# The MLP norm's factor applied with the ReLU by one vector instruction, and paired products that read the input times the norm's weights alone

## The chip, the cores and the metric

The kernel runs on one core of one Trainium2 chip. The metric is the time of one execution on the device in microseconds (us). The kernel before was timed three times; the profiled execution is one more.

## The reference

A decoder trunk of two layers on one sequence of 512 tokens with 1024 features. Each layer has a mixer half and an MLP half; the change lies in the MLP half.

```
def rms_norm(x, g):
    y = xf * lax.rsqrt(jnp.mean(xf * xf, axis=-1, keepdims=True) + NORM_EPS)
    return (y * g.astype(jnp.float32)).astype(x.dtype)
...
for l in range(DEPTH):
    h = rms_norm(x, norm_mix_g[l])
    proj = h @ w_in[l]
    ...
    x = x + mixed @ w_out[l]
    h = rms_norm(x, norm_mlp_g[l])
    x = x + jnp.square(jax.nn.relu(h @ w_mlp_up[l])) @ w_mlp_down[l]
return rms_norm(x, final_norm_g)
```

`mixed` puts together differential attention (6 heads), a short convolution and RWKV-7 (6 heads). `w_mlp_up` is 1024 x 4096, `w_mlp_down` 4096 x 1024. The norm's factor is one positive number for each token, `norm_mlp_g` one number for each feature.

## The kernel before

**Storage and precision.** Activations are kept transposed: `x[j]`, j = 0 to 7, are eight tiles of 128 features x 512 tokens in float32. Every product runs in the matmul type fp32r with each operand split into a high and a low part, and takes three matmuls for each 128 rows of the contraction: high weight by high input, high weight by low input, low weight by high input. So each tensor has an instruction that rounds to the high part (on ScalarE, ACT) and one that subtracts it to get the low part (on VectorE, DVE, or GpSimd, POOL). Weights come from memory by DMAs on SyncE's queue as tiles `raw` (128 x 512), and are split into `whi` (ACT) and `wlo` (DVE, in the mixer half on DVE or POOL as a table has it).

**Order of the work.** In the mixer half the order in which instructions are issued is written out in tables. The MLP half is written as plain code in program order. A scheduler with its own cost model then sets the order on each engine, and may put instructions of the MLP half ahead of instructions that were issued before them, where their inputs and their buffers allow it.

**The end of the mixer half.** The output projection makes eight tiles `po`, in two cuts of four steps of the contraction. DVE adds each to `x[j]` (L715). Of each finished `x[j]`, ACT makes the square (L738, L741), and DVE or POOL, by a table, adds the squares up in `accf` (L744). ACT makes `ahif[j]`, the high part of `x[j]` times the norm's weights (L730), and DVE the low part `alof[j]` (L731). These 16 tiles are the input of the up products: the norm's factor isn't in them. `inner_norm` (L746 to L761) makes the factor: TensorE (PE) sums `accf` over the features (`pssf`), DVE adds the epsilon and scales (`rsx`, L359), POOL raises to the power -0.5 (`rrf`, L363), PE spreads the result over the partitions (`prbf` in PSUM, L757), and ACT copies it into SBUF (`rs`, L761; the trace names its buffer `rsf`). Before, the code kept both `rs` and its copy in PSUM, `rb`.

**The up stage.** The MLP half has 32 up products of 128 outputs. The first eight (`N_ONE`) are ordinary: 24 matmuls of 128 x 512 each, `up_0` to `up_7`. The first three of them are issued with the mixer half. `up(i)` multiplies the sums in PSUM by the norm's factor (`c = up * rs`, DVE, L1402), and `square` takes the ReLU (ACT, L1389) and the square (ACT, L1391). `kept` splits that into `mh` (ACT, L1381) and `ml` (POOL, L1382).

**Inputs of the paired products.** The other 24 up products are made in twelve pairs. For them, during the up stage, `scaled_by_norm(j)` makes `bn[j]`, the normed input: `x[j]` times weights times `rb` (DVE, L1415, reading `rb` from PSUM). `blocks(k)` makes of `bn[k]` and `bn[k + 4]` four sums `t` on halves of the tokens (DVE, L1421 to L1424) and splits them into `thi` (ACT, L1428) and `tlo` (DVE, L1429). `parts_of(j)`, called in the first down products, splits `bn[j]` into `bhi` (ACT, L1437) and `blo` (DVE, L1438). These go into the buffers of `ahif` and `alof`, and so must wait until the last ordinary up product has read those.

**The paired stage.** `two(i0, i1)` makes two up products at once from seven block products in place of eight, each of 12 matmuls of 128 x 256 (a Strassen scheme in Winograd's form: `pa`, `pb`, `pc` are their sums in PSUM). Sums of weight blocks (`s1` to `s4`, DVE, L1458) are split by `both` (ACT L1452, DVE L1453). Three of the products read halves of the normed input (`blk`, from `bhi`/`blo`), four the sums (`smm`, from `thi`/`tlo`). DVE puts the results together into `c0` and `c1`, and `square` is called for the first product of the pair with `[c0]` and for the second with `[pa, c1]`.

**The down products.** `down(h, js)` contracts four squared tiles: for each of eight `j`, 12 matmuls of 128 x 512 into a bank `dn` of PSUM, and DVE adds them to `x[j]` (L1514). After each pair four of these stand in program order, so that a pair and 48 matmuls of `down` make one step. The last part of layer 1 is made by `last_group` (`dnF`).

Of the kernel before, what the change touches and what calls it, by code (L numbers as in the profile page):

```python
# [10 lines left out]
F32 = mybir.dt.float32  # L11
F32R = mybir.dt.float32r
# [3 lines left out]
AF = mybir.ActivationFunctionType  # L16
ALU = mybir.AluOpType
# [5 lines left out]
S = 512  # L23
P = 128
NK = D // P
# [153 lines left out]
N_ONE = 8  # L179
# [7 lines left out]
C_GMIX, C_GMLP, C_SUB, C_CONV, C_MU = 0, 8, 16, 17, 23  # L187
# [81 lines left out]
def tile_trunk(ctx: ExitStack, tc: tile.TileContext, xT, wts, prm_d, cst_d, lora_d, gup_d, lam_d, fin_d, out):  # L269
    nc = tc.nc  # L270
    act, dve, pool = nc.scalar, nc.vector, nc.gpsimd
# [22 lines left out]
    cp = Pool(ctx.enter_context(tc.tile_pool(name="cp", bufs=1)), "cp")  # L294
# [10 lines left out]
    x = [cp.tile([P, S], F32, tag=f"x{j}", name=f"x{j}") for j in range(NK)]  # L305
# [58 lines left out]
    nrm = {}  # L364
# [28 lines left out]
    acts = {}  # L393
# [169 lines left out]
    for l in range(L):  # L563
        pr = prm[l]
# [4 lines left out]
        with ExitStack() as mx:  # L569
# [176 lines left out]
            def inner_norm():  # L746
                key = f"f{l}"
                yield from got(nrm, "all" + key)
                pt = psum("rp", 4, f"pss{key}")
                for b in range(NB):  # L750
                    ins = pe.matmul(pt[:, b:b + 1], nrm[key][0][:, b * P:(b + 1) * P], ones1, start=True, stop=True)
                yield ins
                r = cp.tile([P, NB], F32, tag="rr", bufs=2, name=f"rr{key}")
                yield from root_steps(r, pt[:, :NB], NB)
                rb = psum("rp", 4, f"prb{key}")
                for b in range(NB):
                    ins = pe.matmul(rb[:, b * P:(b + 1) * P], r[:, b:b + 1].to_broadcast([P, P]), ident, start=True, stop=True)  # L757
                yield ins
                rs = cp.tile([P, S], F32, tag="rs", bufs=1, name=f"rs{key}")
                nrm["rs"] = rs, rb  # L760
                yield act.copy(rs, rb)  # L761

            def norm():
# [604 lines left out]
        with ExitStack() as mx:  # L1368
# [2 lines left out]
            H = S // 2  # L1371
            mids = []

            rs, rb = nrm["rs"]

            def kept(m):

# [7 lines left out]
            def square(cs, name):  # L1385

                r = fp.tile([P, S], F32, tag="r", bufs=2, name=f"r{name}")
                for i, c in enumerate(cs):
                    act.activation(r[:, i * H:i * H + c.shape[1]], c, AF.Relu)  # L1389
                m = fp.tile([P, S], F32, tag="m", bufs=3, name=f"m{name}")  # L1390
                act.activation(m, r, AF.Square)  # L1391
                kept(m)

            def up(i):

                if i < NUP:
                    pt = ups[i]
                else:
                    pt = psum("rp", 4, f"up{l}_{i}")
                    mm3(pt, weights(wbase + NG_IN + NG_OUT + i), acts)  # L1400
                c = fp.tile([P, S], F32, tag="c0", bufs=2, name=f"c{l}_{i}")
                dve.tensor_tensor(c, pt, rs, ALU.mult)  # L1402
                square([c], f"{l}_{i}")

            bn, th = {}, {}

            def scaled_by_norm(j):
                if j == 0:  # L1410
                    fp.tile([P, 8], F32, tag="pad0", name=f"pad0_{l}")
                bn[j] = fp.tile([P, 2, H], F32, tag="shi" if j < 5 else "slo", bufs=5, name=f"bn{l}_{j}")
                if j == 5:
                    fp.tile([P, 24], F32, tag="pad1", name=f"pad1_{l}")
                dve.scalar_tensor_tensor(bn[j].rearrange("p a s -> p (a s)"), x[j], pr[:, C_GMLP + j:C_GMLP + j + 1], rb,  # L1415
                                         ALU.mult, ALU.mult)

            def blocks(k):
                b1, b2 = bn[k], bn[k + 4]
# [6 lines left out]
                for i in range(2):  # L1426
                    u = slice(2 * i, 2 * i + 2)
                    act.copy(hi[:, u], t[i])  # L1428
                    dve.tensor_tensor(lo[:, u], t[i], hi[:, u].bitcast(F32), ALU.subtract)  # L1429

            bs = {}

            def parts_of(j):

                n = 1 if j < 4 else 2
                hi, lo = bs[j] = [cp.tile([P, 2, H], F32R, tag=f"a{p}{j}", name=f"b{p}{l}_{j}") for p in ("hi", "lo")]
                act.copy(hi[:, :n], bn[j][:, :n])  # L1437
                dve.tensor_tensor(lo[:, :n], bn[j][:, :n], hi[:, :n].bitcast(F32), ALU.subtract)  # L1438

            def two(i0, i1):  # L1440

                n = f"{l}_{i0}"
                wg = wbase + NG_IN + NG_OUT

                def raw(i, a):
                    t = fp.tile([P, 4, P], F32, tag="sraw", bufs=6, name=f"raw{n}_{i}_{a}")
                    nc.sync.dma_start(t.rearrange("p k c -> p (k c)"), wts[wg + i, :, a * P:(a + 4) * P])
                    return t

                def both(src, name):  # L1450
                    hi, lo = [fp.tile([P, 4, P], F32R, tag=f"s{p}", bufs=5, name=f"s{p}{n}_{name}") for p in ("hi", "lo")]
                    act.copy(hi, src)  # L1452
                    dve.tensor_tensor(lo, src, hi.bitcast(F32), ALU.subtract)  # L1453
                    return hi, lo

                def sum_(name, a, b, op):
                    t = fp.tile([P, 4, P], F32, tag=name, name=f"{name}{n}")
                    dve.tensor_tensor(t, a, b, op)  # L1458
                    return t

                def small(name):
                    return fp.tile([P, H], F32, tag=name, bufs=2, name=f"{name}{n}")

                def product(pt, w, moving, first=True):

                    whi, wlo = w
                    for k in range(4):
                        ahi, alo = moving(k)
                        pe.matmul(pt, whi[:, k], ahi, start=(first and k == 0), stop=False, skip_group_check=True)
                        pe.matmul(pt, whi[:, k], alo, start=False, stop=False, skip_group_check=True)  # L1470
                        pe.matmul(pt, wlo[:, k], ahi, start=False, stop=(k == 3), skip_group_check=True)

                blk = lambda d, q: lambda k: [p[:, q] for p in bs[4 * d + k]]
                smm = lambda q: lambda k: [p[:, q] for p in th[k]]
                pa, pb = [psum("rp", 4, f"p{i}{n}")[:, :H] for i in "ab"]
                pc = psum("at", 2, f"pc{n}")[:, :H]
                c0 = fp.tile([P, S], F32, tag="c0", bufs=2, name=f"c0{n}")
                w11 = raw(i0, 0)
                product(pa, both(w11, "p1"), blk(0, 0))
                p1 = small("p1")  # L1480
                act.copy(p1, pa)
                w21 = raw(i1, 0)
                w22 = raw(i1, 4)
                s1 = sum_("s1", w21, w22, ALU.add)
                product(pb, both(s1, "p5"), smm(0))
                p5 = small("p5")
                dve.tensor_copy(p5, pb)
                s2 = sum_("s2", s1, w11, ALU.subtract)
                product(pa, both(s2, "p6"), smm(1), False)
                u2 = small("u2")  # L1490
                act.copy(u2, pa)
                w12 = raw(i0, 4)
                product(pc, both(w12, "p2"), blk(1, 0))
                dve.tensor_tensor(c0[:, :H], pc, p1, ALU.add)
                s3 = sum_("s3", w11, w21, ALU.subtract)
                product(pa, both(s3, "p7"), smm(2), False)
                c1 = small("c1")
                dve.tensor_tensor(c1, pa, p5, ALU.add)
                s4 = sum_("s4", w12, s2, ALU.subtract)
                product(pb, both(s4, "p3"), blk(1, 1), False)  # L1500
                dve.tensor_tensor(c0[:, H:], pb, u2, ALU.add)
                square([c0], f"{n}_0")
                product(pa, both(w22, "p4"), smm(3), False)
                square([pa, c1], f"{n}_1")

            def down(h, js):

                g, k0 = h // 2, 4 * (h % 2)
                for j in js:
                    pt = psum("mm", 2, f"dn{l}_{h}_{j}")  # L1510
                    mm3(pt, weights(wbase + NG_IN + NG_OUT + NG_UP + 8 * g + j, k0, k0 + 4), mids[4 * h:4 * h + 4], 4)
                    if h == 0:
                        parts_of(j)
                    dve.tensor_tensor(x[j], pt, x[j], ALU.add)  # L1514
                    if h == 2 * N_KG - 1 and j < NK - LATE:
                        norm_tile(j, f"m{l + 1}")


            for i in range(N_ONE):
                up(i)  # L1520
                for j in range(2 * max(i - 2, 0), min(2 * max(i - 1, 0), NK)):
                    scaled_by_norm(j)
                if i >= N_ONE - 4:
                    blocks(i - N_ONE + 4)
            down(0, range(NK))
            h, half = 1, 0
            for p in range(N_TWO):
# [76 lines left out]
```

## Time and profile before

| what | value |
|---|---|
| time before, median of 3 | 1255.2 us (1253.98 to 1256.6) |
| time of the profiled execution | 1255.07 us |
| its span in the trace | 1253.1 us |
| granted TensorE clock, mean | 0.997 |
| moved by DMA | 127.92 MB, 102 GB/s |
| one paired step (a pair and 48 `dn` matmuls) | 21.0 us |

The page lists for each engine its busy time and share of the span. In rows of the trace the first number is the start in us from the span's start, the second the duration; then come engine, line, operation and the tiles, written as out<-in. A bracket at the end of a row gives the idle time of the engine just before it and the instruction that ended that time. In lists of waits each line gives the waiting group, what it waited for, the total in us, the number of waits and the longest one. The ordinary up products of layer 0 run from about 281 to 325 us and those of layer 1 from about 897 to 946; the twelve steps with pairs of layer 1 run from 968 to 1197.

### The profile page before, as it was taken

The numbers are of one execution on the slowest core, as the hardware profiler recorded it, in microseconds if no ns is written. First come the engines' busy times: TensorE is split into PE (matmuls) and PEld (weight loads), VectorE is DVE, ScalarE is ACT, GpSimd is POOL, SyncE is SP. The second block draws the span as 40 slices with busy tenths as digits, with TensorE's granted clock in tenths as the row PEclk, the third lists the DMA queues.
The fourth block names the chain that finished last, engine by engine and source line by source line (L and its number), as shares of the span: only waits on it lengthen the run. The fifth ranks groups of instructions, "written<-read, shape, count | busy, mean of one in ns | idle before, by whom it ended". The sixth has DMA issues, their size and how long they took to land. (4 is left out here: it accounts for less than half of the span.)

```text
span 1253.1 us, 25011 instructions
## 1 busy us (share of the span) xinstructions
PE 1233.6 (98%) x9493; PEld 1055.0 (84%) x9493; DVE 903.3 (72%) x1731; ACT 697.5 (56%) x1476; POOL 358.2 (29%) x461
## 2 busy tenths in 40 slices
PE   9999999999999999999999999999999999999997
PEld 6888788788799999999778887888878999998987
DVE  6887888768967676764666777887598666666654
ACT  6785655546645454544475656464565545454553
POOL 1264637332301010101225455464221111111100
PEclk9999999999999999999999999999999999999998
DMA  6523323142332323221235233232423232323122
GB/s 214 162 91 93 113 87 107 53 143 84 128 100 94 110 93 110 93 93 35 78 109 161 80 119 108 91 88 71 141 84 135 93 109 94 108 95 108 53 76 76
DMA packets 84696, 127.92 MB, mean 102 GB/s; under 512 B 21472, under 2 KB 25568, under 8 KB 84576
## 3 DMA queue, kind: packets, MB, share of 16 engines
q1 hardware_dynamic: 83856, 125.77, 31.4%
q8 instruction: 75, 1.23, 0.4%
q10 hardware_dynamic: 720, 0.55, 0.1%
q14 instruction: 45, 0.37, 0.1%
HBM read 117.11 MB, written 9.18 MB: 101 GB/s over the span
## 5 line engine op out<-in xcount | busy, mean ns | idle before, releaser
L1382 POOL TENSOR_TENSOR ml<-m,mh 128x512 fp32r<-128x512 f32 x64 | 93.4, 1461 | 500.7 <-ACT mh L1381 482.7
L338 ACT CAST whi<-raw 128x512 fp32r<-128x512 f32 x142 | 88.0, 621 | 174.4 <-PE dn L282 159.0
L282 PE MATMUL dn<-mh,whi 128*128 128x512 f32 x448 | 175.1, 391 | 1.2 <-DVE x L1514 1.2
L282 PE MATMUL dn<-ml,whi 128*128 128x512 f32 x448 | 174.6, 390 | 0.0
L282 PE MATMUL dn<-mh,wlo 128*128 128x512 f32 x448 | 174.6, 390 | 0.0
L674 POOL TENSOR_TENSOR wlo<-raw,whi 128x512 fp32r<-128x512 f32 x84 | 110.5, 1316 | 189.2 <-ACT whi L662 159.4
L282 PE MATMUL pj<-ahim,whi 128*128 128x512 f32 x392 | 156.6, 399 | 1.0 <-DVE x L1514 0.9
L282 PE MATMUL pj<-ahim,wlo 128*128 128x512 f32 x392 | 156.7, 400 | 0.0
L282 PE MATMUL pj<-alom,whi 128*128 128x512 f32 x392 | 156.0, 398 | 0.0
L662 ACT CAST whi<-raw 128x512 fp32r<-128x512 f32 x142 | 87.5, 617 | 85.8 <-PE pj L282 29.8
L1514 DVE TENSOR_TENSOR x<-dn,x 128x512 f32<-128x512 f32 x112 | 76.7, 686 | 77.4 <-PE dn L282 77.4
L339 DVE TENSOR_TENSOR wlo<-raw,whi 128x512 fp32r<-128x512 f32 x142 | 113.4, 799 | 11.3 <-ACT whi L338 10.7
L1453 DVE TENSOR_TENSOR slo_p<-s,shi_p 128x512 fp32r<-128x512 f32 x96 | 70.9, 741 | 63.4 <-ACT shi_p L1452 60.8
L282 PEld LDWEIGHTS dn<-mh,whi 128*128 128x128 f32 x448 | 84.1, 188 | 19.9 <-issue 2.0
L282 PEld LDWEIGHTS dn<-mh,wlo 128*128 128x128 f32 x448 | 84.1, 188 | 17.9
L282 PEld LDWEIGHTS dn<-ml,whi 128*128 128x128 f32 x448 | 84.1, 188 | 16.5
L1452 ACT CAST shi_p<-s 128x512 fp32r<-128x512 f32 x96 | 59.1, 617 | 49.7 <-PE pa L282 38.1
L282 PEld LDWEIGHTS pj<-ahim,whi 128*128 128x128 f32 x392 | 73.8, 188 | 15.1 <-ACT whi L662 1.3
L282 PEld LDWEIGHTS pj<-alom,whi 128*128 128x128 f32 x392 | 73.9, 189 | 14.0 <-issue 0.5
L282 PEld LDWEIGHTS pj<-ahim,wlo 128*128 128x128 f32 x392 | 73.8, 188 | 14.0 <-DVE wlo L674 0.2
L282 PE MATMUL pa<-tlo,shi_p 128*128 128x256 f32 x288 | 81.4, 282 | 0.0
L282 PE MATMUL pa<-thi,shi_p 128*128 128x256 f32 x288 | 81.2, 282 | 0.0
(416 smaller groups left out, 3232.5 us busy)
## 6 DMA issues: line engine op xcount, KB each, us to landing
raw<-wts SPq DMA_DIRECT2D x389, 256.0 KB, 2.7
qs<-dqhi SPq DMA_DIRECT2D x24, 128.0 KB, 3.7
ks<-dkhi SPq DMA_DIRECT2D x24, 128.0 KB, 4.0
x<-xT SPq DMA_DIRECT2D x8, 256.0 KB, 4.6
dqhi<-qhi SPq DMA_DIRECT2D x6, 256.0 KB, 3.3
dqlo<-qlo SPq DMA_DIRECT2D x6, 256.0 KB, 3.4
dkhi<-khi SPq DMA_DIRECT2D x6, 256.0 KB, 2.7
dklo<-klo SPq DMA_DIRECT2D x6, 256.0 KB, 3.5
```

Of the source, the lines that this page charges most:

```text
L282: ins = nc.tensor.matmul(*a, **k)
L338: act.copy(hi[:, :n], raw[:, :n])
L339: (pool if a and lean[0] else dve).tensor_tensor(lo[:, :n], raw[:, :n], hi[:, :n].bitcast(F32), ALU.subtract)
L662: yield act.copy(hi[:, k0:k1], raw[:, k0:k1])
L674: yield eng.tensor_tensor(lo[:, k0:k1], raw[:, k0:k1], hi[:, k0:k1].bitcast(F32), ALU.subtract)
L1382: pool.tensor_tensor(lo, m, hi.bitcast(F32), ALU.subtract)
L1452: act.copy(hi, src)
L1453: dve.tensor_tensor(lo, src, hi.bitcast(F32), ALU.subtract)
L1514: dve.tensor_tensor(x[j], pt, x[j], ALU.add)
```

## The change

- `square` no longer has ACT take the ReLU. One DVE instruction (`scalar_tensor_tensor`) takes the larger of its input and 0 and multiplies by the norm's factor `rs`, straight into `r`. The factor is positive, so ReLU first and factor second give the same as the other way round. ACT's square and everything behind it stay.
- `up` gives the sums in PSUM to `square` directly; its multiplication `c` is gone.
- The input of the paired products no longer has the norm's factor in it. `by_gain(j)` takes the place of `scaled_by_norm(j)`: ACT makes `bn[j]` as `x[j]` times the norm's weights, which needs neither the norm's factor nor `rb` in PSUM. It is called with `blocks`, which itself stays the same. One buffer's place and a padding move (`bn[4]` from `shi` to `slo`).
- `parts_of` is gone: what the products read in `bhi`/`blo` are now halves of `ahif`/`alof`, which hold the same without the factor.
- In a pair `square` now applies the factor to `c0`, `pa` and `c1`: three DVE instructions where ACT took three ReLUs.

```diff
@@ inner_norm
-                nrm["rs"] = rs, rb
+                nrm["rs"] = rs
@@ square
                 for i, c in enumerate(cs):
-                    act.activation(r[:, i * H:i * H + c.shape[1]], c, AF.Relu)
+                    q = slice(i * H, i * H + c.shape[1])
+                    dve.scalar_tensor_tensor(r[:, q], c, 0.0, rs[:, q], ALU.max, ALU.mult)
@@ up
-                c = fp.tile([P, S], F32, tag="c0", bufs=2, name=f"c{l}_{i}")
-                dve.tensor_tensor(c, pt, rs, ALU.mult)
-                square([c], f"{l}_{i}")
+                square([pt], f"{l}_{i}")
@@
-            def scaled_by_norm(j):
+            def by_gain(j):
+
                 if j == 0:
                     fp.tile([P, 8], F32, tag="pad0", name=f"pad0_{l}")
-                bn[j] = fp.tile([P, 2, H], F32, tag="shi" if j < 5 else "slo", bufs=5, name=f"bn{l}_{j}")
-                if j == 5:
+                bn[j] = fp.tile([P, 2, H], F32, tag="shi" if j < 4 else "slo", bufs=5, name=f"bn{l}_{j}")
+                if j == 4:
                     fp.tile([P, 24], F32, tag="pad1", name=f"pad1_{l}")
-                dve.scalar_tensor_tensor(bn[j].rearrange("p a s -> p (a s)"), x[j], pr[:, C_GMLP + j:C_GMLP + j + 1], rb,
-                                         ALU.mult, ALU.mult)
+                act.activation(bn[j].rearrange("p a s -> p (a s)"), x[j], AF.Identity, scale=pr[:, C_GMLP + j:C_GMLP + j + 1])
@@
-            def parts_of(j):
-
-                n = 1 if j < 4 else 2
-                hi, lo = bs[j] = [cp.tile([P, 2, H], F32R, tag=f"a{p}{j}", name=f"b{p}{l}_{j}") for p in ("hi", "lo")]
-                act.copy(hi[:, :n], bn[j][:, :n])
-                dve.tensor_tensor(lo[:, :n], bn[j][:, :n], hi[:, :n].bitcast(F32), ALU.subtract)
@@ two
-                blk = lambda d, q: lambda k: [p[:, q] for p in bs[4 * d + k]]
+                blk = lambda d, q: lambda k: [p[:, q * H:(q + 1) * H] for p in acts[4 * d + k]]
@@ down
-                    if h == 0:
-                        parts_of(j)
@@ the loop of the first eight
                 up(i)
-                for j in range(2 * max(i - 2, 0), min(2 * max(i - 1, 0), NK)):
-                    scaled_by_norm(j)
                 if i >= N_ONE - 4:
-                    blocks(i - N_ONE + 4)
+                    k = i - N_ONE + 4
+                    by_gain(k)
+                    by_gain(k + 4)
+                    blocks(k)
```

Besides, the order that the scheduler makes differs: the prediction shows the places on which it rests, in rows of the two programs' instruction order.

More of the change, by code (lines that the diff above doesn't have):

```diff
@@ L1372, in tile_trunk @@
             mids = []
-            rs, rb = nrm["rs"]
+            rs = nrm["rs"]
             def kept(m):
@@ L1429, in blocks @@
                     dve.tensor_tensor(lo[:, u], t[i], hi[:, u].bitcast(F32), ALU.subtract)
-            bs = {}
-            def parts_of(j):
-                n = 1 if j < 4 else 2
-                hi, lo = bs[j] = [cp.tile([P, 2, H], F32R, tag=f"a{p}{j}", name=f"b{p}{l}_{j}") for p in ("hi", "lo")]
-                act.copy(hi[:, :n], bn[j][:, :n])
-                dve.tensor_tensor(lo[:, :n], bn[j][:, :n], hi[:, :n].bitcast(F32), ALU.subtract)
             def two(i0, i1):
```

## The prediction

> **What bounds the kernel now.** I read the page's busy times first, then the waits of PE, then PE row by row where a wait stands.
>
> ```profile
> PE 1233.6 (98%) x9493; PEld 1055.0 (84%) x9493; DVE 903.3 (72%) x1731; ACT 697.5 (56%) x1476; POOL 358.2 (29%) x461
> ```
> ```profile
> PE dn L282 <- DVE x L1514: 1.2, 3, 0.7
> ...
> PE up L282 <- DVE wlo L339: 0.9, 1, 0.9
> ...
> PE up L282 <- ACT whi L338: 0.5, 1, 0.5
> ...
> PE up L282 <- DVE bn L1415: 0.4, 1, 0.4
> ```
> TensorE is busy for 98% of the span, so an edit elsewhere counts only where PE then waits less or more. The second fence (total us, times, longest) holds the waits that the edited code could touch: three in the up products of layer 1, and one of 0.7 in layer 0's first down products, where DVE is late with `x` while it makes the `blo` parts. The change can win little more than these. Their full cost includes the slow restart of PE:
>
> ```profile
> 915.38 0.39 PE L282 MATMUL up<-alof,whi 128*128 128x512 f32 x1
> 915.61 0.39 PE L282 MATMUL up<-ahif,wlo 128*128 128x512 f32 x1
> 916.53 0.50 PE L282 MATMUL up<-ahif,whi 128*128 128x512 f32 x1 [0.53 <-ACT whi L338]
> 916.86 0.40 PE L282 MATMUL up<-alof,whi 128*128 128x512 f32 x1
> 918.14 0.50 PE L282 MATMUL up<-ahif,wlo 128*128 128x512 f32 x1 [0.88 <-DVE wlo L339]
> ...
> 920.32 0.39 PE L282 MATMUL up<-ahif,wlo 128*128 128x512 f32 x1
> 921.09 0.47 PE L282 MATMUL up<-ahif,whi 128*128 128x512 f32 x1 [0.38 <-DVE bn L1415]
> 921.40 0.40 PE L282 MATMUL up<-alof,whi 128*128 128x512 f32 x1
> ```
> Undisturbed matmuls start 0.23 apart. From 915.61 to 921.40 there are 14 steps, worth 3.2; they took 5.8, so **2.6 us** are lost here.
>
> **The change, part by part.** *The paired stage (two thirds of the MLP).* Each pair gains three vector instructions `r` and loses three ReLUs on ACT.
>
> ```profile
> 970.00:1180.00 210.00, 210.00 (x1329) 190.84 (x1328) 143.81 (x232) 104.56 (x201) 27.33 (x20) 1.00 0.30 99
> ```
> ```profile
> L731 DVE SCALAR_TENSOR_TENSOR alof<-x,prm,ahif x16: 743/746/1752, 263.4 to 902.1; 128x512 fp32r<-128x512 f32 x16
> ...
> L730 ACT ACTIVATE ahif<-x,prm x16: 707/710/726, 262.6 to 901.0; 128x512 fp32r<-128x512 f32 x16
> ```
> ```profile
> L1402 DVE TENSOR_TENSOR c<-up,rsf x16: 675/679/692, 291.8 to 947.3; 128x512 f32<-128x512 f32 x16
> ```
> Columns of the first: stretch, its length, then busy time of PE, PEld, DVE, ACT, POOL. In ten steps of 21.0 us PE never idles, and DVE has 66.2 us free, 6.6 a step. The new `r` has no row; its nearest are `alof` (0.75) and `c` (0.68), so a whole one and two half ones take at most 1.5 a step, and fit. Cost 0; ACT's relief is worth 0 as well. The first eight up products trade `c` plus a ReLU for one `r` of `c`'s size: 0. On the path this costs something only without cover, between the last two pairs of layer 1, where no down group stands: at most 1.5.
>
> *What is taken from the up stage.* Eight `bn` and eight `blo` instructions leave DVE there, and the sums `t`/`tlo` move to earlier places. The PE queue of layer 1 moves with them; first before, then after, at the end of the third up product:
>
> ```order
> L282 MATMUL up_2_11687<-ahif_7_11627,wlo_4_11673 128x512
> L282 MATMUL up_4_11803<-ahif_0_11418,whi_0_11806 128x512
> L282 MATMUL up_4_11803<-alof_0_11419,whi_0_11806 128x512
> L282 MATMUL up_4_11803<-ahif_0_11418,wlo_0_11807 128x512
> L282 MATMUL up_4_11803<-ahif_1_11446,whi_0_11806 128x512
> ```
> ```order
> L282 MATMUL up_2_11639<-ahif_7_11579,wlo_4_11625 128x512
> L282 MATMUL up_3_11693<-ahif_0_11370,whi_0_11696 128x512
> L282 MATMUL up_3_11693<-alof_0_11371,whi_0_11696 128x512
> L282 MATMUL up_3_11693<-ahif_0_11370,wlo_0_11697 128x512
> L282 MATMUL up_3_11693<-ahif_1_11398,whi_0_11696 128x512
> ```
> Half of `up_4`, whose weights were not split yet, no longer stands ahead of `up_3`, and no `bn` holds the bank of `prbf`. I count both layers' stalls as won: **-2.6** and, with 0.1 of restart, **-0.8**.
>
> *What is put ahead of the up stage.* In layer 1, DVE's rows between the last additions of the output projection (`x`) and the first `alof`, before and after; `t`, `tlo` are the sums for the pairs, `thi_1` comes from ACT:
>
> ```order
> L715 TENSOR_TENSOR x_74<-po_5_4_11509,x_74 128x512
> L744 TENSOR_TENSOR accf_11416<-accf_11416,sqf_5_11539 128x512
> L715 TENSOR_TENSOR x_75<-po_6_4_11532,x_75 128x512
> L715 TENSOR_TENSOR x_76<-po_7_4_11554,x_76 128x512
> L731 SCALAR_TENSOR_TENSOR alof_2_11573<-x_71,prm_67,ahif_2_11572 128x512
> ```
> ```order
> L715 TENSOR_TENSOR x_75<-po_6_4_11484,x_75 128x512
> L1421 TENSOR_TENSOR t_1_0_11850<-bn_5_11848,t_1_0_11850 128x256
> L1422 TENSOR_TENSOR t_1_1_11851<-bn_5_11848,bn_1_11846 128x256
> L1423 TENSOR_TENSOR t_1_1_11851<-bn_5_11848,t_1_0_11850 128x256
> L1420 TENSOR_TENSOR t_2_0_11911<-bn_2_11907 128x256
> L1428 TENSOR_TENSOR tlo_1_11857<-t_1_0_11850,thi_1_11856 128x512
> L1428 TENSOR_TENSOR tlo_1_11857<-t_1_1_11851,thi_1_11856 128x512
> L715 TENSOR_TENSOR x_76<-po_7_4_11506,x_76 128x512
> L731 SCALAR_TENSOR_TENSOR alof_2_11525<-x_71,prm_67,ahif_2_11524 128x512
> ```
> Six instructions now stand between the last two `x`; `alof_2`, for which PE waits at its third step of `up_0`, stands behind them. POOL's rows there matter too, because DVE and POOL shut each other out:
>
> ```profile
> 315.26 3.99 POOL L1382 TENSOR_TENSOR ml<-m,mh 128x512 fp32r<-128x512 f32 x1 [5.14 <-ACT mh L1381]
> ```
> ```profile
> 315.27 0.68 DVE L1458 TENSOR_TENSOR s<-raw,raw 128x512 f32<-128x512 f32 x1
> ...
> 316.48 0.41 DVE L1424 TENSOR_TENSOR t<-bn,t 128x256 f32<-128x256 f32 x1
> 316.81 0.68 DVE L1429 TENSOR_TENSOR tlo<-t,thi 128x512 fp32r<-128x512 f32 x1
> 317.42 0.68 DVE L1458 TENSOR_TENSOR s<-s,raw 128x512 f32<-128x512 f32 x1
> 318.02 0.68 DVE L1402 TENSOR_TENSOR c<-up,rsf 128x512 f32<-128x512 f32 x1
> 318.62 1.18 DVE L339 TENSOR_TENSOR wlo<-raw,whi 128x512 fp32r<-128x512 f32 x1
> ```
> A POOL instruction that elsewhere takes 1.29 takes 3.99 while DVE runs instructions with two SBUF inputs back to back (0.34 apart for a `t`, 0.60 for a whole tile). It gets through when `c`, which reads PSUM, comes (318.10 + 1.15 = 319.25), and then the next `wlo` is shut out to 319.25 and takes 1.18. `x` reads PSUM as `c` does; `t`, `tlo`, `wlo`, `alof` don't.
>
> ```profile
> 894.28 0.69 DVE L715 TENSOR_TENSOR x<-po,x 128x512 f32<-128x512 f32 x1 [0.36 <-PE po L282]
> 897.00 0.69 DVE L715 TENSOR_TENSOR x<-po,x 128x512 f32<-128x512 f32 x1 [2.03 <-PE po L282]
> 897.61 1.41 DVE L731 SCALAR_TENSOR_TENSOR alof<-x,prm,ahif 128x512 fp32r<-128x512 f32 x2
> ...
> 903.39 0.15 DVE L359 TENSOR_SCALAR rsx<-pssf 128x4 f32<-128x4 f32 x1
> 908.44 0.69 DVE L1402 TENSOR_TENSOR c<-up,rsf 128x512 f32<-128x512 f32 x1 [4.90 <-ACT rsf L761]
> ```
> ```profile
> 894.76 1.29 POOL L674 TENSOR_TENSOR wlo<-raw,whi 128x512 fp32r<-128x512 f32 x1 [1.37 <-ACT whi L662]
> 896.01 1.29 POOL L744 TENSOR_TENSOR accf<-accf,sqf 128x512 f32<-128x512 f32 x1
> 904.31 1.29 POOL L674 TENSOR_TENSOR wlo<-raw,whi 128x512 fp32r<-128x512 f32 x1 [7.01 <-ACT whi L662]
> 905.56 1.02 POOL L363 TENSOR_TENSOR rrf<-rsx,ones 128x4 f32<-128x4 f32 x1
> ```
> Layer 1: `x_6` is on time; POOL's `wlo` shuts the first `t` out to 896.05; four `t` (1.4) and two `tlo` (1.2) end at 898.6, so `x_7` is 1.6 late. There `accf` gets in, to 899.9, and the first `alof` ends at 900.4 in place of 898.3: **+2.1**. PE takes 0.68 a step of three matmuls and DVE 0.67 an `alof`, so nothing is caught up. Ends: +0.5 if nothing is shut out (2.6 of work against 2.0 idle), +3.9 if three POOL instructions (3 x 1.29) each stand in the way.
>
> ```profile
> 278.23 0.69 DVE L715 TENSOR_TENSOR x<-po,x 128x512 f32<-128x512 f32 x1 [1.43 <-PE po L282]
> 278.83 0.68 DVE L674 TENSOR_TENSOR wlo<-raw,whi 128x512 fp32r<-128x512 f32 x1
> 280.95 0.69 DVE L715 TENSOR_TENSOR x<-po,x 128x512 f32<-128x512 f32 x1 [1.43 <-PE po L282]
> ```
> ```profile
> 277.06 1.29 POOL L744 TENSOR_TENSOR accf<-accf,sqf 128x512 f32<-128x512 f32 x1 [1.49 <-ACT sqf L741]
> 279.79 1.29 POOL L744 TENSOR_TENSOR accf<-accf,sqf 128x512 f32<-128x512 f32 x1 [1.43 <-ACT sqf L741]
> ```
> Layer 0 has POOL's `accf` in every step of 2.72. Between the last two `x` now stand `wlo`, four `t` and a `tlo` (2.56) and one `accf` (1.29): 3.85 for the 2.03 there were, +1.8; a second `accf` enters at `x_7` and holds `alof_2` by some 0.8: **+2.6**, with the same ends, 0.5 and 3.9.
>
> *Behind `rsx`, layer 1.* Before, DVE idled there for 4.90 until `c`. Now:
>
> ```order
> L1421 TENSOR_TENSOR t_2_0_11911<-bn_6_11909,t_2_0_11911 128x256
> L1422 TENSOR_TENSOR t_2_1_11912<-bn_6_11909,bn_2_11907 128x256
> L1423 TENSOR_TENSOR t_2_1_11912<-bn_6_11909,t_2_0_11911 128x256
> L1420 TENSOR_TENSOR t_3_0_11972<-bn_3_11968 128x256
> L1428 TENSOR_TENSOR tlo_2_11918<-t_2_0_11911,thi_2_11917 128x512
> L1428 TENSOR_TENSOR tlo_2_11918<-t_2_1_11912,thi_2_11917 128x512
> L1421 TENSOR_TENSOR t_3_0_11972<-bn_7_11970,t_3_0_11972 128x256
> L1422 TENSOR_TENSOR t_3_1_11973<-bn_7_11970,bn_3_11968 128x256
> L1423 TENSOR_TENSOR t_3_1_11973<-bn_7_11970,t_3_0_11972 128x256
> L1443 TENSOR_TENSOR slo_8_p_12151<-raw_8_8_0_12148,shi_8_p_12150 128x512
> L1428 TENSOR_TENSOR tlo_3_11979<-t_3_0_11972,thi_3_11978 128x512
> L1428 TENSOR_TENSOR tlo_3_11979<-t_3_1_11973,thi_3_11978 128x512
> ```
> All twelve read SBUF twice and end 5.5 after `rsx` (7 x 0.34 + 5 x 0.60). POOL's `wlo`, asked for 0.9 after `rsx`, and `rrf` behind it are what the norm waits for:
>
> ```profile
> 906.63 1.16 PE L282 MATMUL prbf<-cst,rrf 128*128 128x128 f32 x8 [0.16 <-POOL rrf L363]
> ```
> `prbf` stands in the PE queue 3.2 after `rsx`, ahead of half of `up_1`. Shut out for the whole run, `wlo` and `rrf` end at 5.5 + 1.29 + 1.02 = 7.8: PE waits **4.6** more. Let in at once: 0. By the row of 3.99, the nearest, I take 4.6. In layer 0 `rrf` has no `wlo` ahead of it and DVE a pause for `whi`: 0.
>
> The Trainium skill, "SBUF — State Buffer", section "SBUF: two separate sides", calls this port pair an exclusive lock that whichever starts first holds for its whole instruction. The row of 3.99 agrees on the lock; by "first come" alone POOL would enter after one DVE instruction, and the sum would be that of the second rival.
>
> **Sum**: -2.6 - 0.8 + 2.1 + 2.6 + 4.6 = +5.9 on the profiled execution's 1255.07 (its span of 1253.1 and 2.0 around it), 0.1 under the median of 1255.2: **1261.0**.
>
> **Rivals.** *The cover holds*: DVE and POOL don't collide at the new places; 0.5 twice, against 3.4 won: -2.4 to -2.9 with the small waits of PE, 1252.2 to 1252.7, faster. For it: the stalls won are measured, and POOL works only 29%. Against it: the 3.99. It decides at 2.4 of delay for both layers together. *The norm's chain gets in*: a gap in DVE's run, which hangs on ACT's `thi`, lets `wlo` and `rrf` through: 2.1 + 2.6 - 3.4 = +1.3, 1256.4. Against it: two gaps are needed, one for each. *The pairs*: `r` waits for the last product ahead of the next pair's weight parts; without a down group as cover up to 1.5, on top of 5.9: 1262.5. *The change doesn't do what it says* can hardly be: the `bn` on DVE are gone from the order; that ACT is relieved is worth nothing.
>
> **How the numbers follow.** Forecast 0.52, cover holds 0.23, chain gets in 0.20, pairs 0.05. 0.2% is 2.5 us, about what a measurement of this kernel can tell from no change. Of the cover's 0.23, 0.03 fall within it, of the forecast's spread 0.01: faster 0.20, same 0.24, slower 0.56. The bounds reach from 1252.2 to 1264.9 (3.9 twice, 4.6, less 2.6); I leave out the last 0.9 of it: 1252.2 to 1264.0.
>
> **What would show it.** `alof_2` ending 2 or more later against the last `po` matmul in both layers; POOL's `accf` or `wlo` lasting well over 1.29 there; PE waiting 3 to 5 for `rrf` in layer 1; no waits left between `up_2` and `dn`; the paired stage still at 21 a step. A `rrf` that starts within 2.5 of `rsx` would break the largest term; a `t` that runs beside a POOL row at 0.41 would break all of the delay.

## The result and the profile after

The changed kernel takes **1262.48 us** (median of 11 runs, 1256.65 to 1267.89) against 1254.65 before (11 runs on the same chip, 1252.72 to 1256.6): ratio 1.0056, 95% interval 1.0037 to 1.0074. It is slower. Its profiled execution took 1261.97, its span is 1260.1: 7.0 more than before.

The page after, busy times; then the waits of TensorE (PE) that are new or changed (total us, times, longest):

```profile
PE 1236.3 (98%) x9493; PEld 1058.1 (84%) x9493; DVE 922.8 (73%) x1771; ACT 667.4 (53%) x1388; POOL 371.7 (30%) x461
```
```profile
PE up L282 <- DVE alof L731: 3.9, 2, 2.0
...
PE up L282 <- ACT ahif L730: 1.4, 2, 0.8
...
PE prbf L282 <- POOL rrf L363: 0.6, 1, 0.6
...
PE dn L282 <- DVE x L1502: 0.5, 2, 0.3
PE up L282 <- DVE x L715: 0.4, 1, 0.4
```

The waits for `wlo`, `whi` and `bn` between `up_2` and `dn` are gone, and so is the 0.7 of layer 0's `dn`. New are the waits for `ahif`, `alof` and `x` at the start of the up stages: 5.7 in all. The one for `rrf` was 0.2 and is 0.6. Row by row, PE in layer 0, after:

```profile
281.76 0.40 PE L282 MATMUL up<-ahif,wlo 128*128 128x512 f32 x1
282.90 0.50 PE L282 MATMUL up<-ahif,whi 128*128 128x512 f32 x1 [0.75 <-ACT ahif L730]
285.33 0.79 PE L282 MATMUL up<-alof,whi 128*128 128x512 f32 x1 [1.92 <-DVE alof L731]
285.92 0.63 PE L282 MATMUL up<-ahif,wlo 128*128 128x512 f32 x1
286.35 0.63 PE L282 MATMUL up<-ahif,whi 128*128 128x512 f32 x1
...
289.01 0.48 PE L282 MATMUL up<-alof,whi 128*128 128x512 f32 x1
289.33 0.39 PE L282 MATMUL up<-ahif,wlo 128*128 128x512 f32 x1
```

Two things are to be seen. PE waits 2.67 for the third step: 0.75 for ACT's `ahif_2`, ahead of which a `thi` of the sums now stands in ACT's queue as well, and then 1.92 for DVE's `alof_2`. And behind the wait its matmuls start 0.43 apart in place of 0.23, until 289. The busy times by stretches of 1 us of the changed kernel tell why; after the stretch and its length stand PE, PEld, DVE, ACT and POOL, and behind them the granted clock:

```profile
284.00:285.00 1.00, 0.00 (x0) 0.00 (x0) 1.00 (x3) 0.29 (x1) 0.00 (x0) 0.97 0.00 0
285.00:286.00 1.00, 0.67 (x2) 0.58 (x3) 1.00 (x3) 1.00 (x3) 0.00 (x0) 0.50 0.00 0
288.00:289.00 1.00, 1.00 (x9) 0.94 (x8) 0.75 (x2) 1.00 (x3) 0.00 (x0) 0.82 0.60 186
906.00:907.00 1.00, 1.00 (x4) 0.83 (x4) 1.00 (x3) 0.88 (x2) 0.00 (x0) 0.59 0.00 0
907.00:908.00 1.00, 1.00 (x6) 0.91 (x6) 1.00 (x3) 1.00 (x3) 0.00 (x0) 0.50 0.00 0
912.00:913.00 1.00, 1.00 (x4) 0.81 (x3) 0.00 (x0) 0.00 (x0) 0.00 (x0) 0.50 0.25 90
913.00:914.00 1.00, 1.00 (x6) 0.79 (x6) 0.00 (x0) 0.69 (x2) 0.00 (x0) 1.00 0.00 0
```

The clock falls to 0.50. From the shares of the edge stretches (0.97 is 0.06 at half, 0.82 is 0.36, 0.59 is 0.82) it was halved from 284.94 to 288.36 and from 906.18 to 913.00: 3.42 and 6.82 us. What that costs is read from the same matmuls of `up_0` before and after. In layer 1 they are these, before, then after:

```profile
898.41 0.50 PE L282 MATMUL up<-alof,whi 128*128 128x512 f32 x1
...
903.37 0.39 PE L282 MATMUL up<-ahif,wlo 128*128 128x512 f32 x1
```
```profile
905.20 0.50 PE L282 MATMUL up<-alof,whi 128*128 128x512 f32 x1 [2.02 <-DVE alof L731]
...
913.06 0.39 PE L282 MATMUL up<-ahif,wlo 128*128 128x512 f32 x1
```

From the first row to the second PE took 4.96 before and 7.86 after, so 2.9 more. In layer 0 it is 3.68 (285.33 to 289.01) for 2.53, so 1.15 more. That is 4.1 that no term of the prediction holds.

The place of the loss, by PE's marks in us from the span's start (end: the span):

| mark | before | after | later by |
|---|---|---|---|
| first `up_0`, layer 0 | 280.75 | 280.52 | -0.23 |
| first `pa`, layer 0 | 349.75 | 352.48 | 2.73 |
| first `up_0`, layer 1 | 896.80 | 900.40 | 3.60 |
| first `pa`, layer 1 | 967.50 | 974.96 | 7.46 |
| first `dnF` | 1196.77 | 1204.22 | 7.45 |
| end | 1253.1 | 1260.1 | 7.0 |

The whole loss lies in the two up stages (2.96 and 3.86) and just ahead of the second (0.87, 0.40 of it the wait for `x`). The twelve paired steps of layer 1 take the same 229.27 and 229.26.

The clock also orders the runs. The three runs with a mean clock of 0.998 took 1256.65, 1257.51 and 1258.28, the one with 0.989 took 1267.89. The clock's difference is worth 0.009 x 1266 = 11.4; the measured one is 10.4. **Where the clock stays up the change costs some 3 us against the median before, and the rest depends on whether the clock falls in that run.**

### The profile page after: what moved, and what is told of

Same layout as the page of the kernel before. It is cut to its first block, busy times and chain, and to the rows that moved or that the text cites. A ratio compares the mean times of both kernels' runs of the same rounds, so it can differ in the third digit from the quotient of the medians.

```text
span 1260.1 us, 24944 instructions
## 1 busy us (share of the span) xinstructions
PE 1236.3 (98%) x9493; PEld 1058.1 (84%) x9493; DVE 922.8 (73%) x1771; ACT 667.4 (53%) x1388; POOL 371.7 (30%) x461
## 5 line engine op out<-in xcount | busy, mean ns | idle before, releaser
L1382 POOL TENSOR_TENSOR ml<-m,mh 128x512 fp32r<-128x512 f32 x64 | 105.0, 1656 | 484.9 <-ACT mh L1381 449.7
L1443 DVE TENSOR_TENSOR slo_p<-s,shi_p 128x512 fp32r<-128x512 f32 x96 | 67.9, 708 | 18.1 <-ACT shi_p L1442 15.5
```

The costliest lines, as they stand in the source:

```text
L1382: pool.tensor_tensor(lo, m, hi.bitcast(F32), ALU.subtract)
```

## The experiments

Three theories. **A**: the sums put ahead of `alof_2` make PE wait, and the wait makes the clock fall to half behind it. **B**: the waits alone, those of the prediction, the one for `rrf` included. **C**: the loss is the new `r` itself, in the ups or the pairs.

**1. All sums behind the norm's factor.** A bias of zero, made from `rs`, so that no `bn` can be made early:

```diff
+    dve.tensor_scalar(zero[0][:, :4], rs[:, :4], 0.0, 0.0, ALU.mult, ALU.add)
-    act.activation(bn[j]..., x[j], AF.Identity, scale=...)
+    act.activation(bn[j]..., x[j], AF.Identity, bias=zero[0][:, :1], scale=...)
```

> The changed kernel, but by_gain gets a bias that is zero and made from rs, so that no bn, t or tlo can be made before the norm's factor is there; everything else of the change stays. Theory A (the loss is TensorE's wait behind the sums that were put ahead of alof_2, and the halved clock after it): both go, the won stalls of the up stage stay won: 1251.5 to 1253.5, clock at least 0.997 in every run, runs within 3 us of each other. Theory B (the wait alone, no part for the clock): the same median, 1251.5 to 1253.5, nothing said of the spread. Theory C (the loss is in the new r instructions of the ups or the pairs): 1259 to 1263.

Measured: 1252.05 (12 runs, 1249.09 to 1254.73), ratio to before 0.9978, interval 0.9967 to 0.9988. In its profile, with a span of 1249.7, PE waits nowhere in the up stages. The level is as expected, and theory C is dead: every `r` of the change is in this kernel, and it is **faster than both**, by 2.8 than before. That is near the 3.4 of stalls that the prediction counted as won. The runs lie 5.6 apart, not 3, with clocks from 0.994: the clock falls at other places too.

**2. TensorE kept busy in its wait.**

```diff
+    if i == 0 and k == 2:
+        fill = psum("at", 2, f"fill{l}")
+        at = piece(NG_IN + NG_OUT, 0)
+        for n in range(FILL):        # 12
+            pe.matmul(fill, his[at][:, 0], inner[0][0], start=(n == 0), stop=(n == FILL - 1))
     operand = yield from got(inner, k)
```

> The changed kernel, with 12 further matmuls of 128x512 in TensorE's queue ahead of the third step of up_0 in each layer, where it idles; their result is not used. Undisturbed they last 12 x 0.227 = 2.7 us. Theory A: TensorE is busy where it idled, the clock stays 1.00 at 281 to 290 and 900 to 915; what is left is the wait: 1256 to 1259, with all runs within 3 us of each other. Theory B: the wait stays as it was and the clock is no matter: 1261 to 1264 with the spread of 11 us as after. Theory C: 1261 to 1264 as well.

Measured: 1266.98 (6 runs, 1263.99 to 1268.39), ratio 1.0092, interval 1.0077 to 1.0107. All three numbers missed. The clock did hold at both places (1.00 in every 2 us from 279 to 295 and 895 to 919, 0.997 in the mean). But the scheduler, which counts on no wait, used the time of the 12 matmuls to put four or five more sums between two `alof`, and in layer 1 the norm came late. PE, DVE and POOL there:

```profile
912.54 0.50 PE L283 MATMUL up<-alof,whi 128*128 128x512 f32 x1 [1.34 <-DVE alof L737]
...
920.11 1.16 PE L283 MATMUL prbf<-cst,rrf 128*128 128x128 f32 x8 [3.39 <-POOL rrf L364]
```
```profile
913.68 0.14 DVE L360 TENSOR_SCALAR rsx<-pssf 128x4 f32<-128x4 f32 x1
...
917.74 1.44 DVE L1434 TENSOR_TENSOR tlo<-t,thi 128x512 fp32r<-128x512 f32 x1 [0.24 <-ACT thi L1433]
```
```profile
914.53 4.10 POOL L675 TENSOR_TENSOR wlo<-raw,whi 128x512 fp32r<-128x512 f32 x1 [10.32 <-ACT whi L663]
918.59 1.47 POOL L364 TENSOR_TENSOR rrf<-rsx,ones 128x4 f32<-128x4 f32 x1
```

`wlo` takes 4.10 for 1.29 while DVE runs sums, and gets in at DVE's first gap, the 0.24 ahead of 917.74. That is the mechanism of the prediction's third term, 3.39 for 4.6, in another order of the sums and with the clock up. The kernel mixes two effects, so experiments 5 to 10 separate them.

**3 and 4. The parts.** In the third kernel the first eight ups are as before and only the pairs have the new input; in the fourth only the first eight have `r`.

```diff
 # third, in up() of the changed kernel
-    square([pt], f"{l}_{i}")
+    dve.tensor_tensor(c, pt, rs, ALU.mult)
+    act.activation(r, c, AF.Relu)
 # fourth, in up() of the kernel before
-    dve.tensor_tensor(c, pt, rs, ALU.mult)
-    square([c], f"{l}_{i}")
+    dve.scalar_tensor_tensor(r, pt, 0.0, rs, ALU.max, ALU.mult)
```

> The changed kernel with the first eight up products as before (c on DVE, ReLU on ACT); only the paired products have the new input and r. Theories A and B: the sums still stand ahead of alof_2, so 1257 to 1268 from run to run, median 1261 to 1264. Theory C, if the ups' r is to blame: 1253 to 1255.

> The kernel before with r in one DVE instruction for the first eight up products alone; the pairs read the normed input and have ACT's ReLU as before. Theories A and B: nothing stands ahead of alof_2, so as before: 1253.5 to 1255.5, runs within 4 us. Theory C: 2 to 8 us more.

Measured: inputs alone 1260.93 (11 runs, 1256.63 to 1265.61), ratio 1.0052, interval 1.0036 to 1.0067; ups alone 1255.94 (12 runs, 1254.44 to 1258.72), ratio 1.0014, interval 1.0005 to 1.0024. Nearly all of the loss comes with the input of the pairs. `r` in the ups alone is no gain: it costs 1.1, and its median lies 0.4 above what A and B expected. In its profile the waits for `wlo` and `bn` of layer 1 are 1.2 and 0.8 where they were 0.9 and 0.4.

**5 to 8. A wait made to measure.** The kernel before, with additions on DVE that nobody reads, between the last two `x`. The order on every engine is else that of before, so nothing but the wait changes; between six and seven only the added matmuls differ.

```diff
-    yield dve.tensor_tensor(x[j], pt, x[j], ALU.add)
+    ins = dve.tensor_tensor(x[j], pt, x[j], ALU.add)
+    if k1 == NK and j == NK - 2:
+        idle = psum("at", 2, f"idle{l}")
+        for n in range(BALLAST):     # 3, 6, 6, 6
+            ins = dve.tensor_tensor(idle, x[j], x[j - 1], ALU.add)
+    yield ins
 # seventh: also the 12 matmuls of the second kernel
 # eighth: tensor_tensor(idle, idle if n else x[j], x[j - 1], ALU.add)
```

> The kernel before, with three further DVE additions of two whole SBUF tiles (into a PSUM bank that nobody reads) between the last two additions of po, in each layer: 1.8 of work where DVE idles 1.43 and 2.03 before. Every engine's order is otherwise that of before. Theory A (wait, and a halved clock behind a wait of 2.5 or more): alof_2 is 0.6 to 1.8 late in each layer, too little for the clock: 1256 to 1258.5, clock 0.996 or more. Theory B (wait alone): the same.

> The same with six additions: 3.6 of work, and POOL's accf and wlo shut out or let in between. alof_2 is 2.6 to 3.9 late in each layer. Theory A: the wait, 5 to 7.5 for both layers, and in most runs 1.7 or 3.4 in a layer for 3.4 or 6.8 us at half clock: median 1262 to 1269, runs 5 us or more apart, clock of 0.990 to 0.995 in most, and a stretch at 0.50 in the profile. Theory B: 1259.5 to 1262, clock as before.

> As with six additions, and 12 further matmuls (2.7 us) in TensorE's queue ahead of the third step of up_0 in each layer, where it waits; DVE's order is the same to the row. Theory A: no stretch at half clock at 280 to 300 and 895 to 920, clock as before, and only the wait is left: 1259.5 to 1262.5, 2 to 6 less than without the matmuls, runs within 4 us. Theory B: as without the matmuls or up to 1 more.

> As with six additions, but five of the six read one operand from PSUM in place of SBUF. If DVE and POOL shut each other out only where DVE reads SBUF twice, POOL's accf of 1.29 runs beside them: x_7 or alof_2 about 1.3 earlier in each layer, 2.6 in both, and the clock falls in fewer runs: 1256.5 to 1263 and below the median with six SBUF additions by 2 or more. If there is no such lock: the same as with six SBUF additions, to 1 us.

| kernel | median (range), runs | ratio, interval | clocks | wait for `alof`, both layers |
|---|---|---|---|---|
| 5: three | 1258.66 (1257.0 to 1261.11), 8 | 1.0035, 1.0022 to 1.0047 | 0.994 to 0.998 | 3.3 |
| 6: six | 1268.27 (1265.95 to 1272.07), 6 | 1.0111, 1.0091 to 1.0132 | 0.987 to 0.993 | 7.7 |
| 7: six, and matmuls | 1261.93 (1260.62 to 1266.96), 6 | 1.0063, 1.0045 to 1.0081 | 0.994 to 0.998 | 2.3 |
| 8: six, from PSUM | 1265.49 (1261.09 to 1268.52), 6 | 1.0083, 1.0065 to 1.0102 | 0.990 to 0.994 | 5.8 |

Six and seven are the test of the clock. The wait of PE in six, then in seven, and the clock at the same two stretches, first six, then seven:

```profile
PE up L283 <- DVE alof L737: 7.7, 2, 4.0
```
```profile
PE up L284 <- DVE alof L743: 2.3, 2, 1.3
```
```profile
287.00:289.00 2.00, 2.00 (x9) 1.71 (x7) 2.00 (x4) 1.44 (x3) 0.00 (x0) 0.50 0.13 44
...
911.00:913.00 2.00, 2.00 (x8) 1.71 (x8) 2.00 (x4) 1.58 (x4) 0.00 (x0) 0.50 0.01 2
```
```profile
287.00:289.00 2.00, 1.93 (x13) 1.66 (x13) 2.00 (x4) 2.00 (x4) 0.00 (x0) 1.00 0.07 15
...
911.00:913.00 2.00, 2.00 (x11) 1.62 (x10) 0.00 (x0) 0.29 (x1) 1.64 (x2) 1.00 0.46 131
```

The 24 added matmuls take 5.4; with the 2.3 that is left they fill the same 7.7. So the wait is as long as it was, yet the kernel is 6.3 faster: **work that nobody uses, put into the wait, saves 6.3 us, and that is the clock.** Theory B expected no gain from it, and 1262 at most for six. The 6.3 is a little more than the 2 to 6 that A expected, and one of seven's runs, the 1266.96 at 0.994, lies outside the 4 us.

Eight is the test of the lock between DVE and POOL. The wait falls from 7.7 to 5.8, 0.98 in each layer, and the time by 2.8, to a median 2.5 above the bound that was expected, since the clock still falls. In layer 0, POOL's `accf` is shut out in six and not in eight:

```profile
279.31 1.75 POOL L750 TENSOR_TENSOR accf<-accf,sqf 128x512 f32<-128x512 f32 x1 [1.43 <-ACT sqf L747]
```
```profile
279.30 1.30 POOL L750 TENSOR_TENSOR accf<-accf,sqf 128x512 f32<-128x512 f32 x1 [1.43 <-ACT sqf L747]
```

Five missed its bounds, 1258.66 for at most 1258.5 and a clock down to 0.994 for 0.996. In its profile a wait of 1.8 in layer 1 was enough: the row of 907 to 909 is at 0.50.

```profile
907.00:909.00 2.00, 2.00 (x7) 1.52 (x6) 0.00 (x0) 0.00 (x0) 0.00 (x0) 0.50 0.49 130
```

**9 and 10. The changed kernel without the run behind `rsx`.** The zero bias of the first kernel for `bn` 2, 3, 6 and 7 alone: the sums of k = 0 and 1 still stand ahead of `alof_2`. The tenth has the 12 matmuls as well; its order on DVE differs by the place of one `tlo`, on ACT by that of one `thi`.

```diff
+    bias=zero[0][:, :1] if j % 4 > 1 else 0.0
```

> The changed kernel, with a zero bias made from rs for bn 2, 3, 6 and 7 alone: the sums of k = 0 and 1 still stand ahead of alof_2 (one t fewer than after), but nothing of k = 2 and 3 stands between rsx and the norm's factor any more. Theory A: TensorE waits some 2 to 2.7 in each layer ahead of alof_2 and the clock halves behind it in most runs: 1256 to 1266, median 1258.5 to 1262.5; rrf follows rsx within 3 in layer 1. If the instructions behind rsx were the larger part of the loss, as the prediction had it: 1254 to 1257.

> The same with 12 further matmuls in TensorE's queue ahead of the third step of up_0. Theory A: no stretch at half clock there, the wait alone is left: 1254.5 to 1258, 2 to 5 less than without them, clock 0.996 or more in most runs. Theory B (wait alone): as without them, to 1 us, or more.

Measured: the ninth 1261.74 (5 runs: 1256.78 at a clock of 0.998, the other four 1260.9 to 1262.07 at 0.991 to 0.994), ratio 1.0056, interval 1.0041 to 1.0071; the tenth 1257.85 (12 runs, 1255.83 to 1260.26, clocks 0.995 to 0.998), ratio 1.0025, interval 1.0015 to 1.0035. The ninth's `rsx` and `rrf`, in layer 1:

```profile
908.41 0.15 DVE L359 TENSOR_SCALAR rsx<-pssf 128x4 f32<-128x4 f32 x1
```
```profile
909.32 1.29 POOL L674 TENSOR_TENSOR wlo<-raw,whi 128x512 fp32r<-128x512 f32 x1 [8.37 <-ACT whi L662]
910.56 1.02 POOL L363 TENSOR_TENSOR rrf<-rsx,ones 128x4 f32<-128x4 f32 x1
```

`rrf` follows `rsx` by 2.15, as before the change, and PE does not wait for it. This profile is of the run of 1256.78, with the clock up; the slower four have no profile, but the same order of instructions. By its median the kernel is as slow as the changed one, as A expected. So the run behind `rsx` is not the larger part of the loss. The matmuls bring 3.9 back: in this pair that is the clock's share. The 3.6 over before that remain are the wait, less the stalls won.

## Why the prediction came out near, point by point

1261.0 was forecast and 1262.48 measured, inside the range. The first half of the reasons holds; the largest single term does not, and another of like size that was missing stands in its place. That the total came out near is luck.

- **Stalls won, -2.6 and -0.8: right.** No wait of PE is left between `up_2` and the first `dn` in either layer. The first experiment shows the gain with nothing against it: -2.8.
- **The paired stage, 0: right.** 229.27 and 229.26 us. DVE was free for `r`, as the row of ten steps said.
- **`alof_2` late, +2.6 in layer 0 and +2.1 in layer 1: right in kind, too small.** PE waited 0.75 + 1.92 = 2.67, and 0.68 + 2.02 = 2.70 with 0.40 for `x` before it; with its slow restarts it lost 3.2 in each layer between the first matmul of `up_0` and that of `alof_2`. Against the last matmul of `po`, `alof_2` itself starts 3.5 later than before in layer 0 and 3.8 in layer 1. The step that was off is that the sums stand between the last two `x` alone, and "Layer 1: `x_6` is on time". Two `tlo` stand ahead of `x_6` too, and POOL stretches them. In layer 0, DVE after:

```profile
277.38 2.40 DVE L1428 TENSOR_TENSOR tlo<-t,thi 128x512 fp32r<-128x512 f32 x2
279.70 0.68 DVE L715 TENSOR_TENSOR x<-po,x 128x512 f32<-128x512 f32 x1
```

There `x_6` is 2.0 late against the last `po` matmul, and the second `accf` that the prediction let in behind `x_7` isn't there: that 2.67 lies so near to 2.6 is luck as well. DVE and POOL after, in layer 1:

```profile
895.56 2.39 DVE L1428 TENSOR_TENSOR tlo<-t,thi 128x512 fp32r<-128x512 f32 x2
897.87 1.78 DVE L744 TENSOR_TENSOR accf<-accf,sqf 128x512 f32<-128x512 f32 x1
899.57 0.68 DVE L715 TENSOR_TENSOR x<-po,x 128x512 f32<-128x512 f32 x1
...
901.18 1.50 DVE L1420 TENSOR_TENSOR t<-bn 128x256 f32<-128x256 f32 x1
...
903.81 0.68 DVE L715 TENSOR_TENSOR x<-po,x 128x512 f32<-128x512 f32 x1
904.41 1.40 DVE L731 SCALAR_TENSOR_TENSOR alof<-x,prm,ahif 128x512 fp32r<-128x512 f32 x2
```
```profile
895.68 1.72 POOL L674 TENSOR_TENSOR wlo<-raw,whi 128x512 fp32r<-128x512 f32 x1 [12.91 <-DVE x L715]
897.80 1.30 POOL L674 TENSOR_TENSOR wlo<-raw,whi 128x512 fp32r<-128x512 f32 x1 [0.40 <-ACT whi L662]
901.05 1.34 POOL L744 TENSOR_TENSOR accf<-accf,sqf 128x512 f32<-128x512 f32 x1 [1.95 <-ACT sqf L741]
```

Two `tlo` (1.28 undisturbed) take 2.39 and an `accf` of 0.68 takes 1.78, each beside a `wlo` of POOL. So `x_6` at 899.57 is late already. The lock is as predicted, but it mostly made DVE wait for POOL: three POOL instructions stretched DVE there, each by some 1.1. Experiment 8 shows the lock by itself: where five of the six additions read PSUM in place of one SBUF tile, the six take 4.4 in layer 0 in place of 5.3, beside the same `accf` of POOL.

- **The norm behind `rsx`, +4.6: wrong here.** PE waited 0.61. `rrf` did come late, 5.07 after `rsx` for 2.17 before, but not because DVE's run shut out `wlo`. The rows of DVE, ACT and POOL:

```profile
910.19 0.15 DVE L359 TENSOR_SCALAR rsx<-pssf 128x4 f32<-128x4 f32 x1
...
914.48 1.98 DVE L1428 TENSOR_TENSOR tlo<-t,thi 128x512 fp32r<-128x512 f32 x2 [2.80 <-ACT thi L1427]
```
```profile
913.31 0.62 ACT L662 CAST whi<-raw 128x512 fp32r<-128x512 f32 x1 [3.66 <-issue]
913.83 1.14 ACT L1427 CAST thi<-t 128x512 fp32r<-128x512 f32 x2
```
```profile
914.00 1.30 POOL L674 TENSOR_TENSOR wlo<-raw,whi 128x512 fp32r<-128x512 f32 x1 [11.61 <-ACT whi L662]
915.26 1.47 POOL L363 TENSOR_TENSOR rrf<-rsx,ones 128x4 f32<-128x4 f32 x1
```
```profile
912.68 0.55 PE L282 MATMUL up<-alof,whi 128*128 128x512 f32 x1
```

`wlo` was asked for when `whi` was there, at 913.9, and ran in 1.30. DVE had a gap of 2.80 just there, in which it waited for ACT's `thi`, as the rival "the norm's chain gets in" had it. The steps that failed are "asked for 0.9 after `rsx`" and "shut out for the whole run": ACT started `whi` 3.1 after `rsx`, and `wlo` was not shut out. What ACT waited for the profile doesn't say ("issue" means that it shows nothing). `whi` starts 0.08 after the end, at 913.23, of the last matmul of `up_0` that reads `whi`, which fits a wait for the buffer of that weight part. At half clock the end of `up_0` was late itself. PE, slowed as well, was ready for `prbf` 6.0 after `rsx` in place of 3.2, and `prbf` started 6.6 after it, for the 7.8 that were argued; so it hardly waited. In the second experiment, with the clock up, `wlo` was asked for 0.85 after `rsx`, and PE did wait 3.39. That the changed kernel itself pays this where its clock holds isn't shown: its three runs at 0.998 lie within 1.5 of the ninth kernel's 1256.78, which has no such run behind `rsx`.

- **The clock, not in the sum: 4.1 in the profiled run** (1.15 and 2.9), 6.3 for six additions, 3.9 in experiments 9 and 10. The prediction priced a wait as its length and the restart. Where the clock holds, the changed kernel takes 1256.7 to 1258.3: nearest to the rival in which the norm's chain gets in (1256.4). The median came near the forecast because the clock took about what the norm was to take; nothing in the prediction foresaw that.

The profiled run's 7.0 by PE's rows: +3.21 and +3.19 from the first `up_0` to the matmul of `alof_2`, +1.15 and +2.90 for the clock behind it, -1.40 and -2.23 in the rest of the two up stages (the stalls won, the wait for `rrf` taken off), +0.87 between the layers, and -0.23 and -0.46 ahead of and behind all this. Of the 0.87, 0.40 is the wait for `x`; the rest of it is not traced, nor why layer 0 won 1.40 and not 0.8.

The Trainium skill, "TensorE: Matmul & The Clock Gate", section "Part 1: The HAM clock gate", has a clock gate that halves TensorE's clock after an idle window of about 3.4 us, by a window that runs freely and does not start with the kernel. The halved stretches of 3.42 and 6.82 agree with one and two such windows. A free-running window is borne out as well: the trace has the time of each change of the clock, and in each of the twelve profiles these times lie whole multiples of 3.413 apart (in the changed kernel's 284.95 and 906.17: 182 of them), while from one profile to the next this grid lies elsewhere against the kernel. That the window has to be idle does not agree: in the 3.42 us ahead of 284.94 PE ran for 1.1 (two matmuls of `up_0` and the row of 282.90), and its longest pause there was 1.54.

Cut along this grid, the rows tell which waits hurt. In the up stages of the changed kernel and of the third, fifth, sixth and eighth, the clock fell at the end of a window in which PE was busy for 0.10 to 0.47 of the time. In the ninth kernel's profiled run the same kind of wait was shared out over two windows; the emptiest were busy for 0.50 and 0.55, and the clock stayed up. So whether a wait of some 2 us halves the clock depends on where the grid happens to lie, which would explain why runs of one program differ. It is not the whole rule: a window of 0.45 in the second kernel passed without a fall, and between the layers, where the matmuls are others, the clock fell behind 0.52 to 0.61.

## What to carry to other kernels

Freeing an instruction from a dependency can be a loss: the scheduler may move it ahead of work that the busiest engine is about to wait for, and a fake dependency (here a bias of zero made from `rs`) that holds it back turned this change from +7.8 into -2.8. Price a new wait of TensorE of 2 us or more not at its length alone but at up to nearly twice that, for the clock behind it (here 7.7 of waits cost 6.3 on top). To tell the two apart put unused matmuls into the wait, and compare the instruction order first, since they may move other work as well.

## What the hardware showed that was not expected

- The granted clock fell to exactly 0.50 behind waits of 1.8 to 4.0, for 3.4 or 6.8 us (10.2 in layer 0 of the third kernel), in some executions of a program and not in others. The ninth kernel's profiled run had waits of 0.49 + 1.85 and 0.65 + 1.69 and a clock of 1.00 throughout both up stages. The single wait of 1.8 that was enough, in the fifth kernel, fell into one window.
- Behind the wait in layer 1 the half clock lasted two stretches of 3.4 though PE's rows show it busy throughout. Part of that was `pssf`, eight matmuls of one column in 1.70; whether these count as work for the clock wasn't tried.
- The unevenness of the kernel before (clocks of 0.995 to 0.998 over its runs) has the same look. In its profile the clock falls only at the end, from 1244.9 on; where it falls in its slower runs is open. In the tenth kernel's profile it is between the layers: 0.91 in the 20 us from 620.
